# Parallel heads of a hybrid encoder as coroutines, one stage per 9216 columns of dense products

## Chip, cores and metric

One core of one Trainium2 chip. The metric is the device time of one execution in microseconds (us); lower is better.

## What is computed

One layer of a streaming encoder on 2048 prompt tokens and 32 decode tokens, model width 1024, all in float32:

```python
hn = rmsnorm(h, norm_mix)
qkv, z, ba, u5, cc = split(hn @ w_in)
ya, s_gdn, b_gconv = gdn_mixer(qkv, z, ba, ...)   # gated DeltaNet, 4 heads x 128, causal conv of width 4
yb, s_s5 = s5_mixer(u5, ...)                      # diagonal state space model, 16 groups, then a GLU
yc, b_conv = conformer_conv(cc, ...)              # GLU, depthwise conv of width 31, layer norm, swish
h = h + concat(ya, yb, yc) @ w_out
hf = rmsnorm(h, norm_ffn)
h = h + (silu(hf @ ffn_w1) * (hf @ ffn_w3)) @ ffn_w2
h = h + (p @ pe_w) * sigmoid(h @ pe_gate_w)
y = rmsnorm(h, norm_final)
```

The outputs are y and the new states of the three heads, for the prompt and for the decode tokens.

## The kernel before

The tokens go through in NB = 4 blocks of 512; the last carries the 32 decode tokens too (544). Activations lie with features on the partitions. Each dense product is made of three passes (high part times high, low times high, high times low), so an output tile of 128 x 512 over K chunks of 128 takes 3K matmuls, 24 for K = 8; in the last block every product is cut into two of 272 columns. `load_weight` (L80) brings a weight tile, ScalarE makes its high part (L93), and at a weight's first use GpSimd makes the low part (L95) and stores it, for later blocks to load. Three such tiles are in flight (WB = 3), and three PSUM buffers take the products (`psD`).

There are two phases. `PhaseA.block(b)` projects block b: u5, the conformer's gate and value, q/k/v (`conv`, L583, with the short causal convolution on VectorE), z; it also makes the gates of the DeltaNet (`gates`, L721). `PhaseF.block(b)` does the output projection, the FFN (`hidden`, L1120, and the w2 products, L1147), the gated embedding and the final norm. Its first product needs all three heads' results for block b, which go through DRAM (`mixT`).

The heads are three functions: `conformer_block` (L771; 31 taps for each of two channel groups, L798 to L800), `gdn_group` (L837; two chunks of 128 tokens at once, with a triangular solve of 31 steps on VectorE, L924 to L929; two groups a block, one more for the decode tokens) and `s5_unit` (L412; two blocks at once, four rounds and a GLU).

The program's order on each engine is drawn when it is built: a list scheduler walks a model of time and gives each engine, of the instructions that the model takes to be ready, the one with the lowest priority number. On the chip an engine then keeps to that order and waits where an instruction is not ready yet. The numbers come from three counters (L1198 to L1217): "first" is the lowest, and is what is current in the two blocks' own code and in `load_weight`; "heads" is above it; "later" is the highest. Dense matmuls are always "later" (`dense`, L110), and so are only met when nothing of a lower number is ready. DeltaNet, S5 and conformer of block 0 run under "heads", emitted between the projection blocks (L1326 to L1337); for block 0's second channel group the conformer uses ScalarE and GpSimd (L791 to L797). The heads of block b + 1 run under "later" within FFN block b, where `put` (L1310) says: the conformer ahead of the output projection, DeltaNet ahead of the first hidden group, S5 of blocks 2 and 3 ahead of the fourth hidden group of FFN block 0. Between two such places a head is emitted whole, ahead of all dense products that follow it.

`rms_bcast` (L138) sums squares with matmuls, makes the reciprocal root and spreads it with transposes (`bcast_cols`, L122) to `bc`, by which evictions multiply. SyncE issues all DMAs, in order.

Of the kernel before, what the change touches and what calls it, by code (L numbers as in the profile page):

```python
# [16 lines left out]
P = 128  # L17
# [11 lines left out]
WB = 3  # L29
TWO_PI = 2.0 * math.pi  # L30
# [107 lines left out]
def rms_bcast(G, pool, pspool, tag, ssum, n, dst, rest=False):  # L138
# [18 lines left out]
    bcast_cols(G, pspool, tag, r, n, dst)  # L157
# [254 lines left out]
def s5_unit(G, A, u, wp, pspool):  # L412
# [14 lines left out]
    for jq in range(4):  # L427
# [17 lines left out]


# [18 lines left out]


# [33 lines left out]


# [28 lines left out]
        V.scalar_tensor_tensor(gq[:, jh], t, 1.0, yf, op0=ALU.add, op1=ALU.mult)  # L530
    spc = 512 // NCT
    for j in range(2):
        yb = wp.tile([P, n], F32, tag="yf", name="yb")
        for s0 in range(0, L5, spc):
# [3 lines left out]
            for k in range(2):  # L538
# [5 lines left out]
                                   gq[:, j, c0:c0 + cn].rearrange("p (s c) -> p s c", c=NCT), op0=ALU.add, op1=ALU.mult)  # L544
        for i in range(G.UB):
# [8 lines left out]
class PhaseA:  # L554
# [58 lines left out]
    def block(self, b):  # L613
# [25 lines left out]
        rc, rt = rms_bcast(G, wp, G.psN, "pn", ssum, n, bc, rest=True)  # L639
# [12 lines left out]
        pb = G.psN.tile([P, 512], F32, tag="pn", name="ps_ba")  # L652
        for w in range(4):
            nc.tensor.transpose(pb[:, w * 16:(w + 1) * 16], fb[:, w * P:(w + 1) * P], G.ident[:16, :16])
        if last:
            nc.tensor.transpose(pb[:TS, 64:80], fb[:, BLK:n], G.ident[:16, :16])
        pb3 = pb[:, :80].rearrange("p (w c) -> p w c", c=16)
        ba = wp.tile([P, 4, 8], F32, tag="ba", name="ba")
        bl = wp.tile([P, 5, 8], F32, tag="bl", name="bl")
        nc.scalar.activation(bl[:, :4], pb3[:, :4, 8:], AF.Copy)  # L660
        V.tensor_tensor(ba, pb3[:, :4, :8], bl[:, :4], op=ALU.add)
        V.tensor_tensor(ba, ba, rc[:, :4, None].to_broadcast([P, 4, 8]), op=ALU.mult)
        if last:
            bad = wp.tile([TS, 1, 8], F32, tag="bad", name="bad", bufs=1)
            nc.scalar.activation(bl[:TS, 4], pb3[:TS, 4, 8:], AF.Copy)
            V.tensor_tensor(bad[:, 0], pb3[:TS, 4, :8], bl[:TS, 4], op=ALU.add)
            V.tensor_scalar(bad, bad, rt, None, op0=ALU.mult)
        gates(G, A, wp, G.psN, ba, b * 4, [P, 4, 8], "gp", G.tp_)
        if last:
            gates(G, A, wp, G.psN, bad, 0, [TS, 1, 8], "gd", G.td_)  # L670

        for j in range(2):
# [4 lines left out]
            for c0, cn in chunks_of(n):  # L677
                p_ = dense(G, G.psD, "pd", w, hf, hl_, ks, c0, cn)
                nc.scalar.activation(ur[:, c0:c0 + cn], p_[:, :cn], AF.Copy)
            V.tensor_tensor(u, ur.rearrange("p (c s) -> p s c", s=L5), bc.rearrange("p (c s) -> p s c", s=L5), op=ALU.mult)  # L680
# [3 lines left out]
        for j in range(2):  # L684
# [36 lines left out]
def gates(G, A, wp, pspool, ba, w0, shp, tag, T):  # L721
# [35 lines left out]
    V.tensor_tensor(g, xs, G.nea[:nt, None, :].to_broadcast(sh), op=ALU.mult)  # L757
    g2 = g.rearrange("p w h -> p (w h)")
# [12 lines left out]
def conformer_block(G, A, b, wp, pspool):  # L771
# [690 lines left out]
```

## Time and profile before

| | |
|---|---|
| median of 3 runs | 2929.85 us (2927.37 to 2934.12) |
| the profiled execution, its own time | 2927.05 us |
| its span | 2925.2 us |
| TensorE matmul busy | 2772.5 us, 95% of the span, 15300 instructions |
| VectorE busy | 1757.4 us, 60%, 3781 instructions |
| ScalarE busy | 951.4 us, 33% |
| GpSimd busy | 622.6 us, 21% |
| mean granted TensorE clock | 0.976 of full speed |

Busy is the time in which at least one instruction of an engine runs; idle is the rest of the stretch. The granted clock is the share of full speed that TensorE was given; it has two levels, 1.2 and 2.4 GHz, and a value between is a mean over a stretch. Matmuls are pipelined, so the pace of a run of them is read from start to start, not from the length of one. The profile names an instruction by its line, its engine and the program's tiles, as out<-in. The edges between stages, at 187, 577, 730, 1322, 1858 and 2388 us, are where a projection block gives way to the next, or where the output projection of an FFN block begins.

### The profile page before, as it was taken

To read this page: it belongs to the slowest core of one execution; us is meant where nothing else is said; L and a number is where in the kernel's file an instruction comes from. 1 tells how busy PE (TensorE), PEld (TensorE's weight loads), DVE (VectorE), ACT (ScalarE), POOL (GpSimd) and SP (SyncE) were. 2 spreads that over 40 slices of the span, in tenths; PEclk is the share of its full clock that TensorE was granted. 3 is DMA by queue.
4 is the path that set the end of the run, shared out by engine and by line. 5 is a ranking of instruction groups with operands and counts; after the bars stand their busy time and mean duration, and the time that the engine had idled before them with its cause. 6 is when DMAs were issued, how large, how long until landed. Compare 5 with 4: busy or idle time off the path is not lost.

```text
span 2925.2 us, 40926 instructions
## 1 busy us (share of the span) xinstructions
PE 2772.5 (95%) x15300; PEld 2370.0 (81%) x15300; DVE 1757.4 (60%) x3781; ACT 951.4 (33%) x1413; POOL 622.6 (21%) x512
## 2 busy tenths in 40 slices
PE   7889987999989999999999999999999999999997
PEld 5667855799878877777788887888888789999997
DVE  8977879876765745667664637763635443333343
ACT  4233344433422222234322223432222343222232
POOL 5731245111633434441010100210100010000000
PEclk9999998999999999999999999999999999999998
DMA  6587755666654546557665646765656665555553
GB/s 223 182 264 224 226 177 170 199 210 215 235 166 164 182 152 232 172 174 250 214 189 165 198 152 220 257 197 169 200 159 195 210 232 173 173 173 173 173 184 107
DMA packets 280565, 565.16 MB, mean 193 GB/s; under 512 B 68992, under 2 KB 128528, under 8 KB 280224
## 3 DMA queue, kind: packets, MB, share of 16 engines
q1 hardware_dynamic: 280368, 562.55, 60.0%
q8 instruction: 121, 1.98, 0.3%
q14 instruction: 76, 0.62, 0.1%
HBM read 457.67 MB, written 104.20 MB: 192 GB/s over the span
## 4 chain that ended last, share of the span: by engine, by line
PE 53%; DVE 2%; DMA 1%; ACT 0%; issue 0%; SPq 0%; POOL 0%; DVEq 0%; ACTq 0%; POOLq 0%
PE ps_d L118 48%; PE ps_kk L884 0%; DVE cacc L800 0%; PE ps_q L956 0%; PE ps_z L968 0%; DVE fal L1072 0%; PE ps_o L1021 0%; PE ps_o L1022 0%; PE ps_s L1014 0%; PE ps_ks L996 0%; PE ps_vn L1004 0%; PE ps_glu L539 0%; PE ps_ss L147 0%; PE ps_nrm L857 0%; ACT fah L76 0%
## 5 line engine op out<-in xcount | busy, mean ns | idle before, releaser
L93 ACT ACTIVATE wh_w<-wr_w 128x1024 fp32r<-128x1024 f32 (+1 forms) x272 | 281.2, 1034 | 787.5 <-PE ps_d L118 560.3
L118 PE MATMUL ps_d<-fah,wh_w 128*128 128x512 f32 (+1 forms) x1760 | 378.4, 354 | 5.9 <-DVE hb L1110 2.2
L118 PE MATMUL ps_d<-fah,wl_w 128*128 128x512 f32 (+1 forms) x1760 | 376.4, 353 | 0.0
L118 PE MATMUL ps_d<-fal,wh_w 128*128 128x512 f32 (+1 forms) x1760 | 375.1, 352 | 0.0
L118 PEld LDWEIGHTS ps_d<-fah,wh_w 128*128 128x128 f32 x1760 | 290.8, 189 | 51.3 <-ACT fah L76 3.4
L118 PEld LDWEIGHTS ps_d<-fah,wl_w 128*128 128x128 f32 x1760 | 291.5, 189 | 43.0 <-issue 0.4
L118 PEld LDWEIGHTS ps_d<-fal,wh_w 128*128 128x128 f32 x1760 | 290.9, 188 | 42.9
L1153 DVE TENSOR_TENSOR hb<-hb,ps_d 128x512 f32<-128x512 f32 (+1 forms) x240 | 140.2, 586 | 241.4 <-PE ps_d L118 240.5
L118 PE MATMUL ps_d<-acth,wh_w 128*128 128x512 f32 (+1 forms) x880 | 209.8, 355 | 8.8 <-DVE hb L1153 6.5
L118 PE MATMUL ps_d<-acth,wl_w 128*128 128x512 f32 (+1 forms) x880 | 212.9, 357 | 0.0
L95 POOL TENSOR_TENSOR wl_w<-wr_w,wh_w 128x1024 fp32r<-128x1024 f32 (+1 forms) x68 | 161.0, 2369 | 242.5 <-ACT wh_w L93 238.5
L118 PE MATMUL ps_d<-actl,wh_w 128*128 128x512 f32 (+1 forms) x880 | 211.0, 355 | 0.0
L118 PEld LDWEIGHTS ps_d<-acth,wh_w 128*128 128x128 f32 x880 | 148.0, 188 | 33.8 <-DVE hb L1153 5.1
L118 PEld LDWEIGHTS ps_d<-actl,wh_w 128*128 128x128 f32 x880 | 150.1, 190 | 22.6
L118 PEld LDWEIGHTS ps_d<-acth,wl_w 128*128 128x128 f32 x880 | 150.1, 190 | 22.5 <-issue 0.4
L800 DVE SCALAR_TENSOR_TENSOR cacc<-xc,cc_w,cacc 128x512 f32<-128x512 f32 (+1 forms) x210 | 162.0, 807 | 0.0
L605 DVE SCALAR_TENSOR_TENSOR gacc<-raw,cw,gacc 128x512 f32<-128x512 f32 (+1 forms) x144 | 122.6, 851 | 35.6 <-ACT gacc L603 33.7
L1135 DVE SCALAR_TENSOR_TENSOR fth<-ps_d,bc 128x512 f32<-128x512 f32 (+1 forms) x110 | 64.8, 590 | 129.2 <-PE ps_d L118 129.0
L1130 DVE TENSOR_TENSOR fa<-ps_d,bc 128x512 f32<-128x512 f32 (+1 forms) x110 | 64.7, 589 | 116.8 <-PE ps_d L118 110.9
L1133 DVE SCALAR_TENSOR_TENSOR fa<-fth,fa 128x512 f32<-128x512 f32 (+1 forms) x110 | 88.0, 800 | 63.2 <-ACT fth L1132 62.9
L118 PE MATMUL ps_d<-hh,wh_qkv 128*128 128x512 f32 (+1 forms) x480 | 105.9, 361 | 11.8 <-DVE cx L929 3.9
L118 PE MATMUL ps_d<-hh,wl_qkv 128*128 128x512 f32 (+1 forms) x480 | 110.5, 369 | 2.3 <-POOL wl_qkv L95 2.3
(471 smaller groups left out, 4809.9 us busy)
## 6 DMA issues: line engine op xcount, KB each, us to landing
wr_w<-in_w SPq DMA_DIRECT2D x256, 512.0 KB, 4.2
wl_w<-lo_w SPq DMA_DIRECT2D x192, 512.0 KB, 3.6
lo_w<-wl_w SPq DMA_DIRECT2D x64, 512.0 KB, 3.3
wr_qkv<-in_w_in SPq DMA_DIRECT2D x48, 512.0 KB, 4.9
wl_qkv<-lo_qkv SPq DMA_DIRECT2D x36, 512.0 KB, 4.1
wr_out<-in_w_out SPq DMA_DIRECT2D x32, 512.0 KB, 4.7
wr_gate<-in_pe_gate SPq DMA_DIRECT2D x32, 512.0 KB, 4.0
sild<-gacc SPq DMA_DIRECT2D x48, 256.0 KB, 5.8
```

Source lines behind the costliest of these rows:

```text
L93: nc.scalar.activation(wh, wr, AF.Copy)
L95: nc.gpsimd.tensor_tensor(wl, wr, wh.bitcast(F32), op=ALU.subtract)
L118: nc.tensor.matmul(ps[:, :cn], a[:, i, :], x(k)[:, c0:c0 + cn], start=start and p_ == 0 and i == 0, stop=stop and p_ == 2 and i == K - 1)
L605: V.scalar_tensor_tensor(acc, raw[:, t:t + W], cw[:, m, t:t + 1], acc, op0=ALU.mult, op1=ALU.add)
L800: V.scalar_tensor_tensor(acc[:, j], xc[:, j, t:t + W], cn_.w[:, j, t:t + 1], acc[:, j], op0=ALU.mult, op1=ALU.add)
L1130: V.tensor_tensor(a, p1[:, :cn], bc[:, cs], op=ALU.mult)
L1133: V.scalar_tensor_tensor(a, th, 1.0, a, op0=ALU.add, op1=ALU.mult)
L1135: V.scalar_tensor_tensor(th, p3[:, :cn], 0.5, bc[:, cs], op0=ALU.mult, op1=ALU.mult)
L1153: V.tensor_tensor(hb[m][:, c0:c0 + cn], hb[m][:, c0:c0 + cn], p_[:, :cn], op=ALU.add)
```

## The change

- `conformer_block`, `gdn_group`, `s5_unit` and `gates` become generators. They yield after each stage, with the number of steps for which the next one is to be held back: `yield 1` mostly, `yield 2` behind loads, `yield 3` behind the DMAs that follow the triangular solve.
- Each call of `dense` counts its columns, 3 K cn, and for every STAGE = 9216 of them all running chains are advanced by a step. Stages are emitted under "later", so that a stage stands in number between the dense products around it. What is left at the end of an FFN block, or of the projection, is emitted by `flush`.
- Block 0's conformer and DeltaNet start with projection block 1, its S5 unit with projection block 2, all under "later" and no longer under "heads". In the FFN one chain per block does conformer, then DeltaNet of the next block, and in FFN block 0 the second S5 unit.
- Block 0's conformer does both channel groups on VectorE.
- In the projection the broadcast, the transposes of b/a and the first part of the gates are put under "later", behind the first u5 product; the rest of the gates behind the conformer's products. In the FFN the broadcast goes behind the first w1 product.
- In `gdn_group` the transposes of k (`ps_kt`) are emitted ahead of the product `ps_vn`.

```diff
+STAGE = 9216
@@ def dense
     K = len(ks)
+    G.step(3 * K * cn)
     with G.later():
@@ def rms_bcast
-    bcast_cols(G, pspool, tag, r, n, dst)
+    if dst is not None:
+        bcast_cols(G, pspool, tag, r, n, dst)
@@ def s5_unit: behind the loads of a round, the input products, the scan, the output, the gelu
+        yield 2
...
+        yield 1
...
+        yield 2
...
+        yield 1
...
+        yield 2
@@ and in the GLU
+            yield 1
@@ PhaseA.block
-        rc, rt = rms_bcast(G, wp, G.psN, "pn", ssum, n, bc, rest=True)
+        rc, rt = rms_bcast(G, wp, G.psN, "pn", ssum, n, None, rest=True)
...
-        pb = G.psN.tile([P, 512], F32, tag="pn", name="ps_ba")
...
-        gates(G, A, wp, G.psN, ba, b * 4, [P, 4, 8], "gp", G.tp_)
-        if last:
-            gates(G, A, wp, G.psN, bad, 0, [TS, 1, 8], "gd", G.td_)
 
         for j in range(2):
             w = load_weight(G, A.w_in[16 + j], KD, "u5", j)
...
                 nc.scalar.activation(ur[:, c0:c0 + cn], p_[:, :cn], AF.Copy)
+            if j == 0:
+
+                with G.later():
+                    bcast_cols(G, G.psN, "pn", rc, n, bc)
+                    pb = G.psN.tile([P, 512], F32, tag="pn", name="ps_ba")
...
+                    gs = [gates(G, A, wp, G.psN, ba, b * 4, [P, 4, 8], "gp", G.tp_)]
+                    if last:
+                        gs.append(gates(G, A, wp, G.psN, bad, 0, [TS, 1, 8], "gd", G.td_))
+                    for g in gs:
+                        next(g)
...
+        with G.later():
+            for g in gs:
+                for _ in g:
+                    pass
         for h in range(NH):
             self.conv(4 + h, 2 * h, b, hf, hl_, bc, n, last, t0)
@@ gates
     V.tensor_tensor(g, xs, G.nea[:nt, None, :].to_broadcast(sh), op=ALU.mult)
+    yield
@@ conformer_block
     for j in range(2):
-        if j and b == 0:
-            nc.scalar.activation(acc[:, j], xc[:, j, 0:W], AF.Identity, scale=cn_.w[:, j, 0:1], bias=cn_.b[:, j:j + 1])
-            for t in range(1, TAPS):
-                pr = wp.tile([P, W], F32, tag="cpr", name="cpr", bufs=2)
-                nc.scalar.activation(pr, xc[:, j, t:t + W], AF.Copy, scale=cn_.w[:, j, t:t + 1])
-                nc.gpsimd.tensor_tensor(acc[:, j], acc[:, j], pr, op=ALU.add)
-            continue
         V.tensor_scalar(acc[:, j], xc[:, j, 0:W], cn_.w[:, j, 0:1], cn_.b[:, j:j + 1], op0=ALU.mult, op1=ALU.add)
         for t in range(1, TAPS):
             V.scalar_tensor_tensor(acc[:, j], xc[:, j, t:t + W], cn_.w[:, j, t:t + 1], acc[:, j], op0=ALU.mult, op1=ALU.add)
+            if t % 6 == 0:
+                yield 1
...
+        if w % 2:
+            yield 1
...
+    yield 2
@@ gdn_group: behind the loads 2; in each chunk's decay and kk part 2 and 1; behind vt 1; behind the solve's loads 2
@@ in the solve, and behind its write back
+        if j % 10 == 9:
+            yield 1
...
+    yield 3
@@ then 1 behind each step of the doubling (5), 3 in each chunk of the recurrence, 1 in each chunk of the output
@@ PhaseF.block
-    def block(self, b, part):
+    def block(self, b):
-        part(-1)
...
-        rms_bcast(G, wp, G.psN, "pn", ssum, n, bc)
+        rc, _ = rms_bcast(G, wp, G.psN, "pn", ssum, n, None)
...
                 p1 = dense(G, G.psD, "pd", w1, lambda k: fh[k], lambda k: fl[k], ks, c0, cn)
+                if j == 0 and c0 == 0:
+                    with G.later():
+                        bcast_cols(G, G.psN, "pn", rc, n, bc)
@@ trunk_kernel
+    G.chains = []
+    G.acc = 0
+
+    def advance(c):
+
+        if c[1] > 1:
+            c[1] -= 1
+            return True
+        with at("later"):
+            c[1] = next(c[0], 0)
+        return c[1] > 0
+
+    def step(cols):
+
+        G.acc += cols
+        while G.acc >= STAGE:
+            G.acc -= STAGE
+            G.chains = [c for c in G.chains if advance(c)]
+
+    def flush():
+        while G.chains:
+            G.chains = [c for c in G.chains if advance(c)]
...
+            G.start(run(conf_of(0), gdn_of(0)))
+            for b in range(1, NB):
+                if b == G.UB:
+                    G.start(s5_unit(G, A, 0, w5, G.psM))
                 pa.block(b)
...
+            G.flush()
     pf = PhaseF(G, A, ctx)
     for b in range(NB):
...
+        nb = b + 1
+        if nb < NB:
+
+            G.start(run(conf_of(nb), gdn_of(nb), *(s5_of(u) for u in range(1, G.NU) if max(u * G.UB - 2, 0) == b)))
+        pf.block(b)
+        G.flush()
```

## Rows read from the trace of the kernel before

**Rows 1.** Busy time by stage: stretch and length; each engine's busy us (instructions); clock; DMA.
```profile
0.00:187.00 187.00, 149.10 (x631) 114.62 (x632) 165.28 (x400) 66.39 (x99) 105.02 (x110) 0.93 0.66 217
187.00:577.00 390.00, 345.50 (x1711) 275.24 (x1710) 318.39 (x704) 159.46 (x257) 124.01 (x132) 0.94 0.65 203
577.00:730.00 153.00, 147.33 (x1152) 144.32 (x1151) 104.29 (x256) 54.06 (x87) 20.39 (x56) 0.99 0.67 213
730.00:1322.00 592.00, 558.81 (x2668) 458.42 (x2667) 378.88 (x687) 174.51 (x249) 261.66 (x133) 0.97 0.57 186
1322.00:1858.00 536.00, 526.76 (x2505) 431.06 (x2504) 325.65 (x667) 171.36 (x244) 40.88 (x31) 1.00 0.62 197
1858.00:2388.00 530.00, 529.31 (x2566) 433.66 (x2565) 262.47 (x651) 171.22 (x247) 47.63 (x38) 1.00 0.63 197
2388.00:2926.00 538.00, 515.65 (x4077) 512.63 (x4075) 202.42 (x421) 154.36 (x235) 22.97 (x16) 0.98 0.52 172
```

**Rows 2.** TensorE in order of time: start, length, line, tiles, count (FFN block 1).
```profile
1566.56 0.85 PE L118 MATMUL ps_d<-fal,wh_w 128*128 128x512 f32 x3
1567.25 1.05 PE L1004 MATMUL ps_vn<-rk,X 128*128 128x128 f32 x8
1568.14 0.60 PE L1009 MATMUL ps_kt<-ident,kq 128*128 128x128 f32 x4
```

**Rows 3.** Dense matmuls alone (L118), by stage: stretch, length, busy (count), clock, DMA.
```profile
187.00:577.00 390.00, 272.10 (x1055) 0.94 0.65 203
730.00:1322.00 592.00, 492.65 (x2016) 0.97 0.57 186
```

**Rows 4.** TensorE's waits, 187 to 730: who <- for whom: us, times, longest.
```profile
PE ps_ct L809 <- DVE cacc L800: 7.8, 1, 7.8
...
PE ps_d L118 <- DVE cgth L692: 5.8, 2, 4.5
PE ps_gc L760 <- DVE g_g L757: 4.2, 1, 4.2
PE ps_bc L130 <- DVE rso L69: 4.2, 1, 4.2
...
PE ps_kk L884 <- ACT eg L877: 0.2, 1, 0.2
```

**Rows 5.** TensorE's waits in projection block 0, 0 to 187.
```profile
PE ps_gc L760 <- issue: 5.2, 1, 5.2
...
PE ps_bc L130 <- issue: 4.2, 1, 4.2
```

**Rows 6.** TensorE's waits in FFN block 0, 730 to 1322.
```profile
PE ps_q L956 <- DVE XT L936: 11.6, 2, 7.7
PE ps_d L118 <- DVE hb L1153: 9.0, 4, 3.5
```

**Rows 7.** Taps by line: count, ns min/median/max, first and last start in us.
```profile
L796 POOL TENSOR_TENSOR cacc<-cacc,cpr x30: 1269/1462/1907, 420.8 to 498.4; 128x512 f32<-128x512 f32 x30
...
L800 DVE SCALAR_TENSOR_TENSOR cacc<-xc,cc_w,cacc x90: 730/746/1841, 423.6 to 611.9; 128x512 f32<-128x512 f32 x90
```

**Rows 8.** GpSimd, then VectorE, in order of time, near 1022 us.
```profile
1021.82 2.39 POOL L95 TENSOR_TENSOR wl_w<-wr_w,wh_w 128x1024 fp32r<-128x1024 f32 x1 [5.10 <-ACT wh_w L93]
...
1021.88 2.37 DVE L929 TENSOR_TENSOR cx<-cx,ct 128x24 f32<-128x24 f32 x1
...
1024.49 0.18 DVE L929 TENSOR_TENSOR cx<-cx,ct 128x16 f32<-128x16 f32 x1
```

**Rows 9.** DeltaNet's first and last work: block 0 (two lines), then block 2.
```profile
L884 PE MATMUL ps_kk<-kq x32: 377/379/764, 193.6 to 378.6; 128*128 128x256 f32 x32
L1046 DVE SCALAR_TENSOR_TENSOR zy<-ps_ot,gnw,zy x4: 735/742/751, 349.5 to 607.4; 128x512 f32<-128x512 f32 x4
...
L884 PE MATMUL ps_kk<-kq x32: 377/379/382, 1467.5 to 1638.3; 128*128 128x256 f32 x32
...
L1046 DVE SCALAR_TENSOR_TENSOR zy<-ps_ot,gnw,zy x4: 751/751/753, 1607.9 to 1772.2; 128x512 f32<-128x512 f32 x4
```

More of the change, by code (lines that the diff above doesn't have):

```diff
@@ L679, in block @@
                 nc.scalar.activation(ur[:, c0:c0 + cn], p_[:, :cn], AF.Copy)
+            if j == 0:
+                with G.later():
+                    bcast_cols(G, G.psN, "pn", rc, n, bc)
+                    pb = G.psN.tile([P, 512], F32, tag="pn", name="ps_ba")
+                    for w in range(4):
+                        nc.tensor.transpose(pb[:, w * 16:(w + 1) * 16], fb[:, w * P:(w + 1) * P], G.ident[:16, :16])
+                    if last:
+                        nc.tensor.transpose(pb[:TS, 64:80], fb[:, BLK:n], G.ident[:16, :16])
+                    pb3 = pb[:, :80].rearrange("p (w c) -> p w c", c=16)
+                    ba = wp.tile([P, 4, 8], F32, tag="ba", name="ba")
+                    bl = wp.tile([P, 5, 8], F32, tag="bl", name="bl")
+                    nc.scalar.activation(bl[:, :4], pb3[:, :4, 8:], AF.Copy)
+                    V.tensor_tensor(ba, pb3[:, :4, :8], bl[:, :4], op=ALU.add)
+                    V.tensor_tensor(ba, ba, rc[:, :4, None].to_broadcast([P, 4, 8]), op=ALU.mult)
+                    if last:
+                        bad = wp.tile([TS, 1, 8], F32, tag="bad", name="bad", bufs=1)
+                        nc.scalar.activation(bl[:TS, 4], pb3[:TS, 4, 8:], AF.Copy)
+                        V.tensor_tensor(bad[:, 0], pb3[:TS, 4, :8], bl[:TS, 4], op=ALU.add)
+                        V.tensor_scalar(bad, bad, rt, None, op0=ALU.mult)
+                    gs = [gates(G, A, wp, G.psN, ba, b * 4, [P, 4, 8], "gp", G.tp_)]
+                    if last:
+                        gs.append(gates(G, A, wp, G.psN, bad, 0, [TS, 1, 8], "gd", G.td_))
+                    for g in gs:
+                        next(g)
             V.tensor_tensor(u, ur.rearrange("p (c s) -> p s c", s=L5), bc.rearrange("p (c s) -> p s c", s=L5), op=ALU.mult)
@@ L1000, in gdn_group @@
             V.scalar_tensor_tensor(R[:, h], pk3[:, h], T.negegc[:nt, tw + w, h:h + 1], vt[:, w, h], op0=ALU.mult, op1=ALU.add)
+        kt = pspool.tile([P, 512], F32, tag="pm", name="ps_kt")
+        for h in range(NH):
+            nc.tensor.transpose(kt[:nt, h * P:(h + 1) * P], kq[:, 2 * h, cw], G.ident)
+        V.tensor_tensor(kd, kt[:nt].rearrange("p (h d) -> p h d", h=NH), T.ekd[:nt, tw + w, :, None].to_broadcast([nt, NH, P]), op=ALU.mult)
+        yield 1
         py = pspool.tile([P, 512], F32, tag="pm", name="ps_vn")
@@ L1006, in gdn_group @@
         V.tensor_tensor(vn, py3, br2[:nt, w, :, None].to_broadcast([nt, NH, P]), op=ALU.mult)
[L1007 to L1010 removed]
+        yield 1
         pn = pspool.tile([P, 512], F32, tag="pm", name="ps_s")
@@ L1141, in block @@
             gr = list(range(g0, min(g0 + NG, HID)))
-            part(g0 // NG)
             for j in gr + [gr[-1] + 1, gr[-1] + 2]:
@@ L1212, in at @@
             tc.cur_priority = G.pr[old]
+    G.chains = []
[15 more added lines that the diff above has]
+            G.chains = [c for c in G.chains if advance(c)]
+    G.step, G.flush = step, flush
+    G.start = lambda g: G.chains.append([g, 0])
     G.first = lambda: at("first")
@@ L1295, in conf_of @@
         with R(f"cc_{b}") as wp:
-            conf(b, wp)
+            yield from conf(b, wp)
     def s5_of(u):
         with R(f"s5_{u}") as wp:
-            s5_unit(G, A, u, wp, G.psM)
+            yield from s5_unit(G, A, u, wp, G.psM)
     def gdn_of(b):
@@ L1304, in gdn_of, with run @@
             for i in range(2):
-                state[0] = gdn_part(b, i, state[0], sp)
-    plan = {}
-    def put(b, place, f, *a):
-        plan.setdefault((b, place), []).append((f, a))
-    for b in range(1, NB):
-        put(b - 1, -1, conf_of, b)
-        put(b - 1, 0, gdn_of, b)
-        if b % G.UB == 0:
-            put(max(b - 2, 0), 3, s5_of, b // G.UB)
+                state[0] = yield from gdn_part(b, i, state[0], sp)
+    def run(*gens):
+        for g in gens:
+            yield from g
     with ExitStack() as cx:
@@ L1326, in trunk_kernel @@
         with R("s5_0") as w5:
-            with R("gd_0", 2) as sp, G.heads():
-                for i in range(2):
-                    state[0] = gdn_part(0, i, state[0], sp)
-            for b in range(1, G.UB):
+            G.start(run(conf_of(0), gdn_of(0)))
+            for b in range(1, NB):
+                if b == G.UB:
+                    G.start(s5_unit(G, A, 0, w5, G.psM))
                 pa.block(b)
-            with G.heads():
-                s5_unit(G, A, 0, w5, G.psM)
-        with R("cc_0") as wp, G.heads():
-            conf(0, wp)
-        for b in range(G.UB, NB):
-            pa.block(b)
+            if NB == G.UB:
+                G.start(s5_unit(G, A, 0, w5, G.psM))
+            G.flush()
     pf = PhaseF(G, A, ctx)
     for b in range(NB):
-        def part(place):
-            with G.later():
-                for f, a in plan.pop((b, place), ()):
-                    f(*a)
-        pf.block(b, part)
-    assert not plan
+        nb = b + 1
[3 more added lines that the diff above has]
+        G.flush()
 def _layout(np, d):
```

35 lines of the change are left out of this document (13 added, 22 removed).

## Prediction

> **What bounds the kernel now.** I read the stretches first: a table of busy time by stage, with the edges set where the projection blocks and the FFN blocks begin [rows 1]. In each stretch TensorE loses time in two ways. It stands idle (length less PE busy), or it works at a granted clock under 1.00, which costs (1 - clock) x length. That gives, idle + clock: projection block 0 (0 to 187) 37.9 + 13.1; projection blocks 1 and 2 (187 to 577) 44.5 + 23.4; block 3 (577 to 730) 5.7 + 1.5; FFN block 0 33.2 + 17.8; FFN block 1 9.2 + 0; FFN block 2 0.7 + 0; FFN block 3 and the tail 22.3 + 10.8. Together 153.5 + 66.6 = 220 us of 2926. The rest is matmul work that the change keeps.
>
> As a control I counted the work. A dense product of 512 columns takes 0.69/3 = 0.23 us, a head's matmul of 128 columns 0.89/8 = 0.111 us, by the starts of three neighbouring rows [rows 2]. From 187 to 577 there are 1055 dense ones [rows 3] and 1711 - 1055 = 656 others: 243 + 73 = 316 us of 390, so 74 are lost, against 68 by the first way. In FFN block 0: 2016 x 0.23 + 652 x 0.111 = 536 of 592, so 56 lost, against 51. Both ways agree, so the kernel is bound by TensorE with holes in it, and nearly all holes lie before 1322 us. VectorE is the next bound: busy 318 of 390 us (82%) in projection blocks 1 and 2, and 379 of 592 (64%) in FFN block 0 [rows 1].
>
> Then I read what ended the holes, in the views of waits. In 187 to 730 there are 17 kinds of wait, led by the conformer's transposes waiting for its taps (7.8), dense products waiting for an eviction (5.8), and the gates' and the broadcast's matmuls (4.2 each); the last is 0.2 [rows 4]. In block 0 the same two cost 5.2 and 4.2 [rows 5]. In FFN block 0 it is the solve's follow-up (11.6) and dense products behind VectorE's add L1153 (9.0) [rows 6]. Such waits exist because the order on an engine is fixed at compile time: a head's matmul that the compiler believed ready holds up all dense work queued behind it.
>
> **Part 1, gates and broadcast put off.** The broadcast transposes and the b/a transposes now stand behind one u5 product, the gates' last part behind all conformer products, and in the FFN the broadcast behind the first w1 product. Their four waits named above sum to 4.2 + 4.2 + 5.2 + 4.2 = 17.8 us. What hides them is dense work: one u5 product is 24 x 0.23 = 5.5 us. On VectorE the first eviction that needs bc now waits for it, and all that VectorE has queued behind it; if the cover were gone, that is up to 5.5 us in 8 places, 44 us. Three product buffers stand against it. I take 15 off.
>
> **Part 2, heads in stages.** A stage is emitted for 9216 columns of dense work, 9216/512 x 0.23 = 4.14 us, with the heads' own matmuls about 4.9. By the yields a conformer has 14 stages, a DeltaNet group of two chunks 30, an S5 unit 32 (34 for the last). So block 0's conformer and DeltaNet need 74, and projection blocks 1 to 3 offer 22 x 12288/9216 x 2 + 31 = 90; FFN block 0 needs 14 + 60 + 34 = 108 and offers 112. They fit. Now every head matmul stands in the queue behind dense work that was asked for earlier, so a late VectorE or DMA step meets dense work in front of it and not behind. That shortens waits for heads [rows 4, 6], but not those for the input splits, and not where a stage lags its turn and is again placed at the moment the compiler thinks it ready. From both sides: nothing, or all of the idle time. The nearest row for the good end is FFN block 2, where the same heads run with 0.7 us idle [rows 1]; for the bad end it is FFN block 0 as it is. I take 60% off: of 187 to 730, (44.5 + 5.7 - 8.4 counted in part 1) x 0.6 = 25; of FFN block 0, 33.2 x 0.6 = 20; of FFN block 1, 4. The heads' DMAs move with their stages on SyncE's queue, between weight loads; FFN block 2 has the same transfers among weight loads at 0.7 us idle, so I take 0.
>
> **Part 3, block 0's conformer.** Thirty adds on GpSimd (median 1.46 us, 44 us in all) and 31 ScalarE steps go; VectorE gets 31 taps of 0.75 us, 23 us [rows 7]. In this trace a GpSimd add holds VectorE up: VectorE's L929 took 2.37 us at 1021.88, beside a GpSimd split that ran for 2.39 us from 1021.82, and 0.18 us at 1024.49 without one [rows 8]. So the 44 us were no free offload. Bounds 23 us more to 44 us less of VectorE; as TensorE is the bound there, I take 0. The Trainium skill, Perfetto Trace Analysis, section Optimizing Scalar/DVE Operations, says that GpSimd and VectorE share an SBUF read port, so that offloading between those two might not help; the trace agrees, by the 2.37 us.
>
> **Part 4, block 1's conformer leaves the projection.** Both of its channels ran with block 0's first, 90 taps from 424 to 612 us [rows 7]; now they start with FFN block 0. VectorE there goes from 379 to about 379 + 62 x 0.75 = 425 of some 570 us, 75%. The splits of low weights on GpSimd, such as the 2.39 us one of [rows 8], stay in that block, with the heads' GpSimd steps queued among them, and keep holding VectorE. Dense products behind VectorE waited 9.0 us there [rows 6]; I add 6.
>
> **Clock.** In the four stretches before 1322 us the clock cost 55.8 us beside 121.3 us idle: 0.46 us per us of idle. Parts 1 and 2 take 15 + 25 + 20 = 60 us of idle away there, so 28 us of clock.
>
> **Sum.** -15 - 25 - 20 - 4 - 28 + 6 = -86 us. The profiled execution took 2927.05 us, 1.85 more than its span of 2925.2; the median of the three runs is 2.8 above it. 2927 - 86 + 3 = **2844 us**.
>
> **Rivals.**
> (a) The order hardly changes. In FFN block 1 the heads of DeltaNet take (1772.2 - 1467.5)/60 = 5.1 us a stage [rows 9], just over the 4.9 us of a step. Heads that lag their turn are issued when ready, as before, and the waits for them stay. Then part 1 and the conformer's 7.8 us remain: 15 + 8 + 0.46 x 23 = 33, time 2897. For it: 5.1 against 4.9. Against it: the early stages, those with several steps allotted for a DMA, and block 0's heads, which lose their higher rank.
> (b) Nearly all holes close, as in FFN block 2: idle left 15 (block 0), 12, 8 and 2, with their clock. Then 121 + 10 - 37 = 94 idle less and 43 of clock, time 2793. Against it: VectorE at 75% and more, and the GpSimd holds.
> (c) Slower: block 0's heads come too late for FFN block 0, whose first product needs them all. The DeltaNet of block 0 takes (607.4 - 193.6)/60 = 6.9 us a stage now [rows 9], ranked ahead of all dense products. It will start 14 stages (69 us) later and rank among them. At 6.9 it ends at 194 + 69 + 414 = 677 us, and the shortened projection at 730 - 1.46 x (15 + 25) = 672, so this is the point from which it decides: each us a stage more is 60 us of idle TensorE, in one hole. At 9 us a stage the hole is 126 us: 2930 - 86 + 126 = 2970. For it: VectorE at 82%, and dense evictions ranked first on it. Against it: VectorE is freed there of block 1's taps (47 us) and of holds (up to 44).
> (d) Cutting the heads finer lowers the clock by itself. In the trace it does not: from 1322 to 2388, where head and dense matmuls alternate, the granted clock is 1.00, its 2.4 GHz level [rows 1]; it fell where idle time came before. If the 0.94 of 187 to 577 came to hold in FFN blocks 1 and 2, they would lose 0.06 x 1066 = 64 us, and the 28 us of clock would not come back: 2844 + 92 = 2936. The Trainium skill, Perfetto Trace Analysis, section Matmul Optimizations, asks that matmuls execute back to back in batches because the engine scales with utilization; read strictly, that speaks for (d), and the 1.00 speaks against it.
>
> **How the numbers follow.** Forecast (2815 to 2872) 0.53; (a) 0.22; (b) 0.15; (c) 0.07; (d) 0.03. The range 2795 to 2905 holds the forecast, nearly all of (a) and half of (b), 0.81. A measurement of this kernel can tell about 0.2%, 6 us, from no change. Faster by more than that: 0.53 + 0.15 + most of (a), 0.89; within it: 0.02; slower: 0.09.
>
> **What would show it.** Right: the out-projection of block 0 starts near 672 us and that of block 1 near 1240; TensorE idle from 187 to there near 20 us; granted clock over 0.97 there; the waits of broadcast, gates and conformer transposes gone. (a): the wait for the solve's result stays near 11 us in FFN block 0. (c): a hole of tens of us ahead of the first out-projection, ended by the DeltaNet's last step or the transfer behind it. Part 3 is wrong if VectorE's busy share in the projection rises over 88%. The whole is wrong if dense products wait for evictions for more than about 30 us, since then VectorE and not the placing of heads made the holes.

## The result, and the profile after

The kernel after takes **2906.34 us** (median of 4 runs, 2906.04 to 2909.94), the kernel before, run beside it, 2929.57: a ratio of 0.9922, 95% interval 0.9904 to 0.9939, or 23 us less, where 86 were forecast. The profiled execution of the kernel after took 2906.6 us with a span of 2904.8.

The stretches of the kernel after, cut where [rows 1] cut those of before (here projection block 0, blocks 1 and 2, block 3, then the four FFN blocks): length, then busy us of PE, PEld, DVE, ACT and POOL, clock, DMA share, GB/s.
```profile
0.00:186.00 186.00, 151.47 (x631) 116.35 (x632) 164.82 (x400) 65.29 (x98) 114.06 (x110) 0.92 0.66 215
186.00:524.00 338.00, 318.74 (x1557) 255.04 (x1555) 273.49 (x614) 134.16 (x208) 94.83 (x102) 0.96 0.73 230
524.00:707.00 183.00, 170.80 (x1310) 162.25 (x1311) 146.05 (x385) 62.30 (x109) 44.48 (x61) 0.97 0.59 189
707.00:1292.00 585.00, 557.65 (x2660) 458.58 (x2659) 388.77 (x676) 170.46 (x243) 256.49 (x125) 0.96 0.57 188
1292.00:1836.00 544.00, 530.32 (x2513) 434.17 (x2512) 311.62 (x645) 174.40 (x250) 46.06 (x33) 0.99 0.61 195
1836.00:2368.00 532.00, 531.23 (x2568) 434.77 (x2567) 282.70 (x675) 171.04 (x247) 47.16 (x38) 1.00 0.62 197
2368.00:2905.00 537.00, 515.36 (x4074) 512.36 (x4072) 201.80 (x421) 153.72 (x234) 22.33 (x16) 0.98 0.53 172
```
Projection blocks 1 and 2 took 390 us and take 338; block 3 took 153 and takes 183. So 52 us were won and 30 of them lost right behind; in part that is work that moved, since TensorE does 154 instructions fewer in the first stretch and 158 more in the second. FFN block 0 won 7, FFN block 1 lost 8. Length less PE busy, summed over the seven rows, is 129.4 us of idle TensorE where [rows 1] had 153.5; the mean granted clock is 0.976 in both. The holes in block 0 and in FFN block 0 are nearly all still there.

TensorE's waits in projection block 0 of the kernel after (who <- for whom: us, times, longest):
```profile
PE ps_gc L780 <- issue: 5.1, 1, 5.1
...
PE ps_bc L132 <- issue: 4.3, 1, 4.3
```
These answer [rows 5] and haven't moved: put off or not, the broadcast and the gates of block 0 are met as early as before (the first ps_gc matmul at 108.2 us, 108.4 before). In FFN block 0:
```profile
PE ps_y L518 <- DVE X L498: 13.7, 3, 5.5
PE ps_q L982 <- DVE XT L961: 4.7, 2, 3.5
PE ps_d L120 <- DVE hb L1187: 4.5, 4, 1.4
```
Against [rows 6] the solve's wait fell from 11.6 to 4.7 us and the dense products' wait for the add from 9.0 to 4.5, but S5's outputs now wait 13.7 us. In the kernel before they waited 7.6:
```profile
PE ps_y L512 <- DVE X L493: 7.6, 3, 3.9
```
The waits are in part handed on.

### The profile page after: what moved, and what is told of

It reads as the page before. It is cut to its first block, busy times and chain, and to the rows that moved or that the text cites. A ratio compares the mean times of both kernels' runs of the same rounds, so it can differ in the third digit from the quotient of the medians.

```text
span 2904.8 us, 40874 instructions
## 1 busy us (share of the span) xinstructions
PE 2775.6 (96%) x15300; PEld 2373.5 (82%) x15300; DVE 1769.2 (61%) x3812; ACT 931.4 (32%) x1382; POOL 625.4 (22%) x482
## 4 chain that ended last, share of the span: by engine, by line
PE 73%; DVE 14%; DMA 8%; issue 2%; SPq 2%; ACT 1%; POOL 0%; DVEq 0%; ACTq 0%; POOLq 0%
PE ps_d L120 65%; DVE gacc L614 1%; DVE cx L952 1%; DMA sild<-gacc 1%; DMA cu<-ud 1%; DVE ct L951 1%; PE ps_q L982 1%; DMA xk<-in_xT 1%; DMA mixT<-zy 1%; PE ps_z L995 1%; DVE cacc L813 1%; PE ps_kk L904 1%; DMA zy<-zgd 1%; DVE X L498 1%; PE ps_ks L1025 1%
## 5 line engine op out<-in xcount | busy, mean ns | idle before, releaser
L813 DVE SCALAR_TENSOR_TENSOR cacc<-xc,cc_w,cacc 128x512 f32<-128x512 f32 (+1 forms) x240 | 178.8, 779 | 0.0
L614 DVE SCALAR_TENSOR_TENSOR gacc<-raw,cw,gacc 128x512 f32<-128x512 f32 (+1 forms) x144 | 118.9, 828 | 27.4 <-ACT gacc L612 24.8
L1173 DVE TENSOR_TENSOR actl<-fa,acth 128x512 fp32r<-128x512 f32 (+1 forms) x110 | 85.5, 778 | 48.6 <-ACT acth L1172 48.4
L120 PE MATMUL ps_d<-hh,wl_qkv 128*128 128x512 f32 (+1 forms) x480 | 108.2, 362 | 5.9 <-POOL wl_qkv L96 5.9
```

Source lines behind the costliest of these rows:

```text
L120: nc.tensor.matmul(ps[:, :cn], a[:, i, :], x(k)[:, c0:c0 + cn], start=start and p_ == 0 and i == 0, stop=stop and p_ == 2 and i == K - 1)
L614: V.scalar_tensor_tensor(acc, raw[:, t:t + W], cw[:, m, t:t + 1], acc, op0=ALU.mult, op1=ALU.add)
L813: V.scalar_tensor_tensor(acc[:, j], xc[:, j, t:t + W], cn_.w[:, j, t:t + 1], acc[:, j], op0=ALU.mult, op1=ALU.add)
L1173: V.tensor_tensor(fb[:, cs], a, fa[:, cs].bitcast(F32), op=ALU.subtract)
```

## Experiments

The table holds their times, the text takes them in the order of the questions. "Of before" is the ratio to the kernel before on the same chip, with its 95% interval; at this length 0.001 is 2.9 us. The two kernels with the copied low part leave out the subtraction, so their results are other numbers.

| kernel | us | of before |
|---|---|---|
| before_conf0: before + part 3 | 2897.9 | 0.9886 [0.9869, 0.9904] |
| before_tapdve: before, adds on VectorE | 2900.5 | 0.9897 [0.9883, 0.9910] |
| before_part1: before + part 1 | 2916.3 | 0.9953 [0.9938, 0.9968] |
| before_conf0_part1: before + parts 1 and 3 | 2901.1 | 0.9899 [0.9886, 0.9913] |
| after_noconf0: after without part 3 | 2932.2 | 1.0007 [0.9998, 1.0017] |
| after_projwhole: after, stages in the FFN alone | 2890.0 | 0.9861 [0.9847, 0.9874] |
| after_ffnwhole: after, stages in the projection alone | 2919.8 | 0.9960 [0.9946, 0.9973] |
| after_projrank: after, stages of the projection ranked as heads | 2901.0 | 0.9904 [0.9886, 0.9921] |
| st4608: after, STAGE 4608 | 2932.7 | 1.0014 [1.0003, 1.0026] |
| st13824: after, STAGE 13824 | 3010.9 | 1.0284 [1.0268, 1.0300] |
| after_copylow: after, low part copied by ScalarE | 2831.1 | 0.9665 [0.9650, 0.9680] |
| before_copylow: before, low part copied by ScalarE | 2845.9 | 0.9717 [0.9704, 0.9729] |
| after_dvesplit: after, split on VectorE | 2845.1 | 0.9708 [0.9691, 0.9725] |
| before_dvesplit: before, split on VectorE | 2857.0 | 0.9752 [0.9739, 0.9766] |
| before_conf0_part1_dvesplit: before + parts 1 and 3, split on VectorE | 2842.6 | 0.9699 [0.9680, 0.9718] |
| after_projwhole_dvesplit: stages in the FFN alone, split on VectorE | 2839.5 | 0.9695 [0.9675, 0.9716] |

### Do the stages bind?

The leading theory after the result (S): the heads are one chain that lags its turns, so the count of columns doesn't bind, that is, it holds nothing back. Its rival (P): the spacing gained the 23 us.
```diff
-STAGE = 9216
+STAGE = 4608
```


> The kernel after with STAGE = 4608: a stage is offered for every 2 us of dense work instead of every 4.1. Theory S (the heads are one serial chain that lags its turns, so the count of columns does not bind): within 0.3% of the kernel after (2898 to 2915 us), and the heads of FFN block 0 at the same times as in the kernel after (kk of block 1's second group near 955 us, S5's outputs from 1148 us). Theory P (the spacing by stages is what gained the 23 us): the gain goes back towards the kernel before, 2920 to 2935 us, and TensorE's waits for the solve's result in FFN block 0 grow from 4.7 us towards 11.6.

It took 2932.7 us: P, by the time. TensorE's waits in its FFN block 0:
```profile
PE ps_y L518 <- DVE X L498: 13.3, 4, 4.3
PE ps_q L982 <- DVE XT L961: 11.2, 2, 7.0
```
The solve's wait is back near the 11.6 us of [rows 6]. The first ps_kk matmul of FFN block 0 starts at 762.6 us, at 771.8 in the kernel after, at 783.6 in the kernel before. These starts have to be counted from where the block begins, at 720, 707 and 730 us: 43, 65 and 54 us into it. In a kernel that emits the whole chain ahead of the block (after_ffnwhole, below) it is 41 us. So S was wrong: stages of 9216 hold the heads back by some 20 us, stages of 4608 by next to nothing.

The other way, a stage half as long again:
```diff
-STAGE = 9216
+STAGE = 13824
```


> The kernel after with STAGE = 13824: a stage is offered for every 6.2 us of dense work, 7.2 with the heads' own matmuls, more than the 5.1 us that a stage of the chain takes. Theory S: stages bind for the first time; with heads now held back behind dense work the waits of dense products for heads (solve 4.7, zz 4.2 and 6.5) fall under 2 us each, but block 0's chain (74 stages at 6.2 to 7.2 us) no longer ends inside the projection, so a hole of 50 to 150 us stands ahead of the first out-projection: 2950 to 3050 us. Theory P (9216 is near the best spacing and the chain is not late): 2905 to 2925 us and no such hole.

It took 3010.9 us, with the hole that S told; S's other mark, waits of dense products for zz under 2 us, was missed, at 14.1 us in all from 187 to 756 us. The hole ahead of the first out-projection, then FFN block 0:
```profile
673.00:756.00 83.00, 31.35 (x187) 26.52 (x185) 41.69 (x115) 12.01 (x28) 8.31 (x8) 0.62 0.19 57
756.00:1280.00 524.00, 520.77 (x2459) 427.80 (x2460) 314.66 (x509) 161.03 (x225) 232.03 (x104) 0.99 0.56 187
```
TensorE's waits in that hole:
```profile
PE ps_ct L824 <- DVE cacc L813: 16.0, 1, 16.0
PE ps_d L120 <- ACT fah L1103: 12.4, 1, 12.4
PE ps_q L982 <- DVE XT L961: 9.2, 1, 9.2
PE ps_ot L1078 <- DVE o L1070: 6.7, 1, 6.7
```
Here stages do bind. From 756 to 1280 TensorE idles 3.2 us only; the price is 52 us of idle in front of it, where block 0's DeltaNet and the next block's conformer are still at work, and stretches of the same kind ahead of the third and the fourth FFN block (1849 to 1886 and 2413 to 2471 us), with 25 and 41 us of idle. In this FFN block 0 DeltaNet does all of its 32 ps_kk matmuls and TensorE never waits for its solve; S5's output matmuls have left the block. The stage that closes the holes is too long for the chain, and the one that fits the chain closes few of them.

### Which part gave the 23 us?

Part 3 alone on the kernel before, and the kernel after without it:
```diff
-        if j and b == 0:
-            nc.scalar.activation(acc[:, j], xc[:, j, 0:W], AF.Identity, scale=cn_.w[:, j, 0:1], bias=cn_.b[:, j:j + 1])
-            for t in range(1, TAPS):
...
-            continue
```


> The kernel before with part 3 alone: block 0's conformer does both channel groups on VectorE; heads stay emitted whole, ranked as before. Theory 3 (the 23 us come from part 3, since GpSimd's thirty adds held VectorE up): 2900 to 2915 us, the projection's blocks 1 to 3 shorter by 15 to 25 us. Theory R (the 23 us come from the new rank and order of the heads): within 8 us of the kernel before, because 31 taps of 0.75 us come onto VectorE and about 28 us of holds go.

> The kernel after without part 3: block 0's second channel group goes back to ScalarE and GpSimd, in the same stages. Theory 3: most of the gain goes, 2922 to 2935 us. Theory R: 2900 to 2912 us.

Part 3 alone gives 33 us, and without it the kernel after is level with the kernel before. Theory 3 holds: without part 3 the rest of the change comes to nothing, gains and losses together. The stretch from 387 to 577 us of the kernel before, where block 0's conformer runs:
```profile
387.00:577.00 190.00, 161.34 (x745) 126.98 (x743) 167.64 (x313) 85.38 (x136) 71.04 (x69) 0.92 0.56 174
```
and of the kernel before with part 3:
```profile
387.00:577.00 190.00, 180.18 (x945) 146.90 (x944) 172.19 (x367) 75.53 (x125) 59.35 (x43) 0.98 0.62 202
```
VectorE does 54 instructions more, and is busy 4.6 us longer. TensorE's idle time falls from 28.7 to 9.8 us and the clock's loss from 15 to 4: together 30 us in this stretch alone (it holds more matmuls too, 945 for 745, since the work runs ahead).

Is it GpSimd's adds that did the harm, or ScalarE's products, or the length of the chain? One word tells:
```diff
-                nc.gpsimd.tensor_tensor(acc[:, j], acc[:, j], pr, op=ALU.add)
+                nc.vector.tensor_tensor(acc[:, j], acc[:, j], pr, op=ALU.add)
```


> The kernel before with one word changed: the thirty adds of block 0's second channel group on VectorE and not on GpSimd; ScalarE still makes the 31 products. If part 3 gains because GpSimd's adds held VectorE: the adds cost VectorE about 0.6 to 0.75 us each, as much as the taps of part 3, and the time is that of part 3 alone within 8 us, 2890 to 2906 us. If it gains by what it takes off ScalarE, or by a shorter chain: 2920 to 2935 us.

2900.5 us, within 3 of part 3 alone, with ScalarE's 31 products still there. So it isn't the products. The chain of adds got shorter too: the conformer's last transpose of block 0 starts at 511 us in the kernel before and at 496 here. But in the kernel before TensorE waits for none of these adds, and what they do to VectorE can be counted: the solve's 62 steps between 387 and 577 us (L928 and L929) are busy 32 us in the kernel before and 15 here. So the adds on GpSimd did it, by what they do to VectorE. What one does, from the kernel before:
```profile
439.64 0.22 DVE L929 TENSOR_TENSOR cx<-cx,ct 128x65 f32<-128x65 f32 x1
...
440.49 1.27 POOL L796 TENSOR_TENSOR cacc<-cacc,cpr 128x512 f32<-128x512 f32 x1 [8.98 <-ACT cpr L795]
440.54 1.30 DVE L928 TENSOR_TENSOR ct<-cx,cu 128x60 f32<-128x60 f32 x1
```
Of two neighbouring steps of the solve, of nearly the same size, the one at 439.64 takes 0.22 us and the one at 440.54 takes 1.30, the length of the add beside it; the median of that line (L928) is 0.215 us. In what follows such an instruction is called held, and its delay a hold.

Part 1 alone (broadcast, b/a transposes and gates put behind a dense product):

> The kernel before with part 1 alone: broadcast, b/a transposes and gates put behind a dense product, heads as before. By the prediction's step: 15 us of idle and 7 us of clock less, 2905 to 2912 us, the waits of ps_bc and ps_gc in block 0 and later under 1 us each. By the traces of before and after (in block 0 both waits stand at the same place on TensorE in both, 4.2 and 5.2 before, 4.3 and 5.1 after): at most 4 to 8 us less, 2922 to 2930 us.

2916.3 us, 14 less: between the two expectations, a little nearer to the prediction's in size, but not in its place, since in block 0 the wait of ps_gc stays at 5.3 us and that of ps_bc at 2.2 (1.9 in before_conf0, which hasn't part 1). On top of part 3 it gives nothing:

> The kernel before with parts 1 and 3 and without the stages: the kernel after less its coroutines. Alone, part 3 gave 32.6 us and part 1 14.2. If both add up: 2880 to 2888 us, and then the stages (part 2) cost 18 to 26 us of the kernel after. Rival: parts 1 and 3 fill the same holes, 2893 to 2900 us, and the stages cost 5 to 13 us. If part 2 gains as the prediction has it, this kernel stands above 2906 us.

2901.1 against 2897.9, intervals overlapping. The rival holds, 1 us outside its range: parts 1 and 3 fill the same holes. From 2901 to the kernel after, the stages with what belongs to them seem to add 5 us, which is not clear of the noise; without part 3 they add 16 (2916 to 2932), which is.

### Where do the stages cost, and where do they give?

Stages in the FFN alone, block 0's heads emitted whole and ranked as heads, as before:
```diff
-            G.start(run(conf_of(0), gdn_of(0)))
-            for b in range(1, NB):
...
+            whole(gdn_of(0))
+            for b in range(1, G.UB):
                 pa.block(b)
...
+            whole(s5_unit(G, A, 0, w5, G.psM))
+        whole(conf_of(0))
+        for b in range(G.UB, NB):
+            pa.block(b)
```


> The kernel after with block 0's heads emitted whole and ranked as heads in the projection, as before (DeltaNet from block 1 on, S5 behind block 1, conformer behind it); stages in the FFN blocks alone. If what the stages cost, they cost in the projection (block 0's heads late and below dense products): 2878 to 2892 us, the out-projection of block 0 at 690 to 697 us and not 707. If they cost it in the FFN blocks: 2900 to 2910 us.

Stages in the projection alone; each chain of the FFN is emitted whole, all of it ahead of the output projection and not at the three places of the kernel before:
```diff
+        G.flush()
         pf.block(b)
-        G.flush()
```


> The kernel after with stages in the projection alone; in the FFN blocks each chain is emitted whole, under the same rank, ahead of the out-projection. If the stages matter in the FFN blocks as the prediction has it (part 2, FFN block 0: 20 us and clock): 2915 to 2935 us and the wait for the solve's result back near 11 us in FFN block 0. If a head is issued when it is ready whatever its stage: within 8 us of the kernel after, 2898 to 2914 us.

2890.0 and 2919.8 us. The four kernels make a square: without stages 2901; in the FFN alone 11 less; in the projection alone 19 more; in both 5 more. One corner is not clean: the 19 hold the new place of the heads in the FFN too. In the FFN blocks the stages do what they are for: with whole heads the waits of FFN block 0 are
```profile
PE ps_q L982 <- DVE XT L961: 12.1, 2, 7.4
PE ps_y L518 <- DVE X L498: 9.6, 3, 5.6
```
against 4.7 and 13.7 with stages. In the projection they cost 16 us (2890 to 2906). From 186 to 707 us TensorE of the kernel after waits longest for
```profile
PE ps_d L120 <- DVE zz L730: 10.7, 3, 4.9
PE ps_q L982 <- DVE g_p L771: 4.2, 1, 4.2
```
and in the kernel with whole heads there (186 to 690 us) for the first of these only
```profile
PE ps_d L120 <- DVE zz L730: 2.3, 1, 2.3
```
Is it the low rank, or the place and order?
```diff
-        with at("later"):
+        with at(G.rank):
```
Here `G.rank` is "heads" in the projection and "later" in the FFN blocks.

> The kernel after; in the projection the stages keep their places and order, but are emitted under heads, above all dense products, and no longer under later. If the low rank costs the 16 us there: 2888 to 2896 us. If the order costs them (conformer first, DeltaNet not before 300 us, S5 beside block 2): 2902 to 2912 us.

2901.0 us, between the two expectations: 5 less than the kernel after, and the intervals of the two overlap. In the profiled execution the projection's blocks 1 to 3 take 526 us, 521 in the kernel after, so the higher rank gains nothing there; what it has less lies in FFN block 0, 576 us for 585. Most of the 16 us is then due to the order (conformer first, DeltaNet from 300 us and not from 194 [rows 9], S5 from block 2 on), but how much is not settled.

### What makes the holes?

Nearly all splits of low weights on GpSimd stand in block 0 and FFN block 0, and so do 62 of the 129 us of idle TensorE that are left. First without the splits' work on GpSimd:
```diff
-            nc.gpsimd.tensor_tensor(wl, wr, wh.bitcast(F32), op=ALU.subtract)
+            nc.scalar.activation(wl, wr, AF.Copy)
```


> The kernel after, but the low part of a weight is made by ScalarE as a copy of the weight, not by GpSimd as the difference to the high part: it leaves out the subtraction (the low passes multiply by the wrong part), and with it all of GpSimd's splits in block 0 and FFN block 0, while the transfers, ScalarE's place in the chain of a weight and TensorE's work stay. Theory H (GpSimd's splits, by holding VectorE for their 2.4 us, make what idle time is left before 1292 us): 50 to 90 us faster than the kernel after, 2815 to 2855 us, waits in FFN block 0 (ps_y 13.7, solve 4.7) gone. Theory S (a serial chain of heads): the holes stay, less than 20 us faster, 2887 to 2907 us. The split itself is then on ScalarE's queue, about 1.2 us each, ahead of evictions there: up to 15 us slower than either says.

> The kernel before with the same edit (low part made by ScalarE as a copy; leaves out the subtraction). Theory H: 60 to 110 us faster than the kernel before, 2820 to 2870 us, and the kernel after with this edit is then less than 10 us from it, since both had the same holds in FFN block 0. If the order of the heads is worth something by itself, the kernel after with this edit stays 20 us or more below this one. Theory S: less than 20 us faster than before, 2910 to 2930 us.

2831 and 2846 us: 75 and 83 less, each against its own kernel. Theory H, on both orders of the heads, though they stand 15 us apart where H allowed 10; before_copylow still has GpSimd's thirty adds. As these kernels multiply other data, the next one keeps the data and only moves the split to VectorE:
```diff
-            nc.gpsimd.tensor_tensor(wl, wr, wh.bitcast(F32), op=ALU.subtract)
+            nc.vector.tensor_tensor(wl, wr, wh.bitcast(F32), op=ALU.subtract)
```


> The kernel after with the low part of a weight made by VectorE itself and not by GpSimd, same values. Theory H (what costs is that a GpSimd split holds VectorE for its whole 2.4 us): VectorE pays its own time for a split, about half of 2.4 us, TensorE's idle time in FFN block 0 falls from 27 to under 15 us, 2840 to 2880 us in all. Rival: the run with the copy on ScalarE gained because VectorE was free of splits altogether (or because of the other data in the low passes); then a split on VectorE, which stands in its fixed order among the heads' steps, costs as much as the hold: 2895 to 2925 us.

2845.1 us, 61 less than the kernel after. By the two profiles, whose spans lie 58 us apart, FFN block 0 is 45 us shorter, projection block 0 26, and projection blocks 1 to 3 are 12 longer. FFN block 0 of it, then TensorE's longest waits there:
```profile
693.00:1233.00 540.00, 534.24 (x2620) 440.58 (x2618) 360.04 (x731) 173.56 (x247) 53.28 (x38) 1.00 0.61 200
```
```profile
PE ps_y L518 <- DVE X L498: 2.7, 1, 2.7
PE ps_v L459 <- DMA c_PT<-s5PTim: 1.7, 1, 1.7
```
Idle 5.8 us where the kernel after has 27.4; clock 1.00 where it has 0.96; the solve's wait is gone. VectorE does 55 instructions more there and is busy 29 us less; over the whole execution it does 108 more, the splits, and is busy 40 us less. Why shows in its instructions by line and form, FFN block 0 of the kernel after (busy us, mean ns | idle before):
```profile
L1168 DVE SCALAR_TENSOR_TENSOR fa<-fth,fa 128x512 f32<-128x512 f32 x22 | 41.5, 1888 | 15.5 <-ACT fth L1167 15.5
L1173 DVE TENSOR_TENSOR actl<-fa,acth 128x512 fp32r<-128x512 f32 x22 | 34.2, 1553 | 12.2 <-ACT acth L1172 12.0
...
L1170 DVE SCALAR_TENSOR_TENSOR fth<-ps_d,bc 128x512 f32<-128x512 f32 x22 | 15.1, 687 | 17.0 <-PE ps_d L120 16.6
```
and the same with the split on VectorE:
```profile
L96 DVE TENSOR_TENSOR wl_w<-wr_w,wh_w 128x1024 fp32r<-128x1024 f32 x64 | 79.1, 1235 | 13.8 <-ACT wh_w L94 13.0 <-DMA lo_w<-wl_w 0.4
...
L1173 DVE TENSOR_TENSOR actl<-fa,acth 128x512 fp32r<-128x512 f32 x22 | 18.7, 849 | 0.0
L1168 DVE SCALAR_TENSOR_TENSOR fa<-fth,fa 128x512 f32<-128x512 f32 x22 | 15.6, 708 | 0.2
...
L1170 DVE SCALAR_TENSOR_TENSOR fth<-ps_d,bc 128x512 f32<-128x512 f32 x22 | 15.1, 688 | 24.3 <-PE ps_d L120 24.3
```
`fa<-fth,fa`, with both tensors in SBUF, fell from 1888 to 708 ns; `fth<-ps_d,bc`, with one of them in PSUM, is 687 and 688. The Trainium skill, SBUF — State Buffer, section Who interferes with whom, says that a VectorE instruction with two SBUF inputs contends with a GpSimd instruction that reads SBUF, that the pair of ports the two engines share is an exclusive lock, and that a VectorE instruction with at most one SBUF input, outside the 2-port modes, doesn't contend. The trace agrees, by 1888 against 708 ns and by 687 against 688.

A split on VectorE is also shorter than one on GpSimd, so weights come sooner. In FFN block 0 of the kernel after that isn't the cause, as TensorE waits for no split there. In projection block 0 it waits 5.9 us for one (ps_d <- POOL wl_qkv), and there the runs don't part the shorter split from the holds.

What are the stages worth when the holds are gone?

> The kernel before with the splits on VectorE, same values. If the holes that part 2 was to close were made by the holds: 50 to 75 us faster than the kernel before, 2855 to 2880 us, the wait for the solve in FFN block 0 under 4 us with the old order of heads. If the old order made them: 2900 to 2925 us, and the kernel after with the same edit (2845) is 55 us or more ahead.

> After_projwhole with the splits on VectorE, same values. If the two edits add up: 2890 - 61 = 2829 us, within 8. If with the holds gone the order of block 0's heads no longer matters: 2840 to 2850 us, as after_dvesplit.

> The kernel before with parts 1 and 3 and the splits on VectorE, no stages, same values. If the stages help the FFN blocks by placing heads well: 2850 us, 10 above after_projwhole_dvesplit (2839.5), as without the splits' edit. If they helped only by softening the holds: 2835 to 2845 us.

2857.0, 2839.5 and 2842.6 us. The old order of heads, with the splits moved, has 5 us of idle in FFN block 0 (544 us, 539.06 busy) and no wait for the solve among its five largest, the largest 1.3 us in all. So it was the holds that made those holes, in the old order as in that of stages of 9216. One word in the kernel before is worth 73 us, three times what the whole change gave. The two edits don't add up: 2839.5 and not 2829. With parts 1 and 3 and without stages the time is 2842.6, with stages in the FFN 2839.5, with stages everywhere 2845.1, all intervals overlapping: without the holds the stages are worth nothing that could be measured. Their 11 us in the FFN blocks were then the softening of holds. Any of the three is some 60 us faster than the kernel after.

## Why the prediction was wrong, by its own steps

**The bound was read rightly, the cause of the holes wrongly.** TensorE with holes in it, nearly all before 1322 us: both kernels show that. But "such waits exist because the order on an engine is fixed at compile time" was half of it. The order met a VectorE that GpSimd held up, by its splits in projection block 0 and FFN block 0 and by its adds in the projection's blocks 1 and 2. (That the compiler's model of time leaves holds out is argued; no trace shows the model.) With the splits moved the old order is good enough in FFN block 0. A view of the kernel before would have told it: VectorE's instructions by line and form, in FFN block 0,
```profile
L1133 DVE SCALAR_TENSOR_TENSOR fa<-fth,fa 128x512 f32<-128x512 f32 x22 | 38.1, 1733 | 12.1 <-ACT fth L1132 12.1
...
L1135 DVE SCALAR_TENSOR_TENSOR fth<-ps_d,bc 128x512 f32<-128x512 f32 x22 | 15.1, 687 | 12.2 <-PE ps_d L118 11.9
```
and in FFN block 1, where there are no splits:
```profile
L1135 DVE SCALAR_TENSOR_TENSOR fth<-ps_d,bc 128x512 f32<-128x512 f32 x22 | 15.2, 690 | 27.9 <-PE ps_d L118 27.9
L1133 DVE SCALAR_TENSOR_TENSOR fa<-fth,fa 128x512 f32<-128x512 f32 x22 | 15.2, 689 | 8.8 <-ACT fth L1132 8.7
```
The same 22 instructions cost 1733 ns in one block and 689 in the next. The prediction had a single case [rows 8], a split's and not an add's, and didn't ask how often it happens.

**Part 1, 15 and its clock, 7.** Alone it gives 14; on top of part 3 nothing. The waits were right, their independence wrong, and in block 0 the waits stood where they were.

**Part 2, 25 + 20 + 4 and clock, 21.** This is the term that failed most. The failed step is the reading of the holes as the order's alone: it took 60% of all idle time as mended by order, by the nearness of FFN block 2; but FFN block 2 differs from FFN block 0 in the splits too. Measured: 11 us won in the FFN blocks, clock and all, and 16 us lost in the projection; the same FFN block 0 went from 33 us of idle to 5 by moving the splits in the old order. That the early stages would meet dense work in front of them holds in FFN block 0 (solve 11.6 to 4.7), but S5 took the time back.

**Part 3, at 0.** The mechanism was named, with the right row, and bounds of 23 more to 44 less; the value was put at 0 "as TensorE is the bound there". That step failed: TensorE's idle time is mostly waits for VectorE, so a hold on VectorE can cost TensorE time although VectorE has time to spare. It gave 33 us alone, more than the whole change gained.

**Part 4, 6 more.** It didn't happen as described. The next block's taps still ran in the projection, from 562 to 641 us, and VectorE in FFN block 0 went from 379 to 389 us and not to 425. The scheduler takes, of what it holds ready, the lowest number, and an idle VectorE takes a tap of any rank; a stage orders only engines that have other work waiting.

**The clock, 28.** The mean is 0.976 in both. With 24 us less idle time and not 60 there was little to come back, and the step's 0.46 us of clock for each us of idle didn't hold either: 11 us would have come back. FFN block 0 lost 6 us of idle and its clock went from 0.97 to 0.96. With the splits on VectorE FFN block 0 rises from 0.96 to 1.00, as the step had it for closed holes.

**The rivals.** (a), 2897, was the nearest in time, by luck: its condition, heads that lag their turns, is refuted by the run with STAGE 4608, its mark, the solve's wait at 11 us in FFN block 0, didn't show, and its 2897 left part 3 out. (b)'s closed holes came about in FFN block 0 alone, and only with the splits moved (5.8 us of idle); no run reached 2793. (c) did not decide at 9216: DeltaNet of block 0 ends near 662 us, 677 were reckoned, and the out-projection starts at 707. At STAGE 13824 it decided, with 52 us of idle in one hole, and the time was 3011. (d) is refuted: the clock is 1.00 in FFN block 2 with stages. Of the marks, the out-projections at 672 and 1240 were missed at 707 and 1292, and the idle time from 187 to the first of them was 31 us and not 20. The mark for a VectorE that makes the holes, evictions awaited for over 30 us, was badly chosen: from 186 to 1292 us dense products wait some 19 us for evictions (zz, raw, cgth, hb), and yet VectorE, held up, made nearly all the holes of FFN block 0.

## What to carry to other kernels

Before the order of an engine's queue is blamed for its waits, compare the mean length of the same instruction between a stage with the holes and one without: a shape that takes 1.7 us here and 0.7 there is being held, and an order can hide a hold but not end it. With STAGE 13824 FFN block 0 had 3 us of idle although `fa<-fth,fa` still took 1720 ns there; the time came back as holes elsewhere. Work on GpSimd isn't free for VectorE when both read two tensors from SBUF; here moving it onto VectorE made VectorE less busy. And a pace for background work needs a stage that the chain can keep and that still makes it wait: here half of 9216 gave back all that the change had gained, and half as much again was too long for the deadlines.

## What the runs showed of the hardware that was not expected

- A split of 128 x 1024 takes 2.43 us on GpSimd and 1.24 us on VectorE, and on GpSimd it holds VectorE besides: FFN block 0's VectorE goes from 388.8 busy us to 360.0 when it does the splits itself, and to 274.3 when ScalarE makes copies in their stead. The last does the same 676 instructions as the first, so the holds there come to 114 us of VectorE.
- Of VectorE's instructions of 512 columns in FFN block 0 only those with both tensors in SBUF were held (1888 against 708 ns on average; the median, 2460, is as long as a split); those that read one from PSUM stayed at 687 ns beside the same splits. Evictions don't suffer there, what follows them does.
- One with a single tensor in SBUF can be held as well: the conformer's first tap (L798) of the kernel before took 1642 ns at 420.8 us, with a GpSimd add beside it, and 547 at the median.
- ScalarE's copy of the same tile took 1.06 us and put nothing in VectorE's way; TensorE's longest wait in that FFN block 0 was 4.3 us, for a DMA.
